# Low parts of weight tiles: an adding DMA in place of subtractions on VectorE and GpSimd

## The chip, the core and the metric

The kernel runs on one core of a Trainium2 chip. The metric is the device time of one execution, in microseconds (us). The profile names the engines: PE is TensorE (matrix products), with PEld for its weight loads; DVE is VectorE, ACT is ScalarE, POOL is GpSimd, and SP is the engine that issues the kernel's DMAs. Each engine works through its own queue in order.

## What is computed

One encoder block over 512 tokens and 16 meta tokens of width 1024, all in float32. Cut to what matters here:

```python
u = rms_norm(h, pre_mix_gain)
proj = u @ w_in                                # 1024 x 6656: qa, ka, va, qb, kb, vb, gates
o_swa  = windowed_gqa_sink_attention(rope(qa), rope(ka), va, sink)      # 16 query heads, 4 of K and V
o_diff = differential_attention(rope(qb), rope(kb), vb, lam)            # 8 heads, two softmaxes each
merged = sigmoid(g0) * (o_swa @ w_branch_swa) + sigmoid(g1) * (o_diff @ w_branch_diff)
h = h + rms_norm(merged @ w_out)
u = rms_norm(h, pre_ffn_gain)
f = (silu(u @ w_gate) * (u @ w_up)) @ w_ffn_out                         # hidden width 2816
out = h + rms_norm(f)
```

## The kernel before

**Two parts for each operand.** TensorE multiplies in a format with fewer mantissa bits (`float32r`). So every operand `x` of a large product is split into a high part, `hi = x` rounded to that format, and a low part, `lo = x - hi`. A product is `hi*hi + hi*lo + lo*hi`, three matmuls that accumulate in one bank (`mm3`, L139, its matmuls on L142, L143 and L144). The weight's low part is the stationary operand of L144.

**Weight tiles.** All weights pass through `load_w` (L124) in tiles of 128 x 1024, 512 KB each: 139 calls. SP issues a DMA from HBM into a raw tile `wr` (L126). ScalarE casts it into the high part `wh` (L130). The low part `wl` is `wr - wh` through `sub_hi` (L110, its instruction on L111). A counter `nw` numbers the calls. Calls 4 to 51 give three quarters of the columns (768) to GpSimd and one quarter (256) to VectorE; all others give all 1024 to VectorE. Raw tiles have `RB = 3` buffers, `wh` and `wl` three each (`wp`, L106). Some tiles have high and low parts of their own: the V tile of the windowed branch, `wV` (call 1), and the last two of each half of the FFN's second product (`xw`). Two tiles for the first K projection (`w_half`) and seven tiles of `w_out` are split by the helper `split` (L113) and not by `load_w`.

**Stages.** First x arrives slice by slice and is split, with the K and V projections of the windowed branch (`wV`, tile 1, then tile 2 for the second half of V). Then attention: streams for the windowed scores, their transposes and value products, the same for the differential branch, and a stream of fillers (projections for Q, K, V, gates, and `w_branch_swa`), which takes one weight tile after the other. `Order` (L35) lays down TensorE's order when the program is made, from fixed costs and delays (`LAT`); it does not depend on what the other engines do in the run. The other engines' orders come from the tile scheduler, except in the opening stage, where those of VectorE, ScalarE and SP follow the text. After attention come the product with `w_branch_diff` (8 tiles), `w_out` (8), the norm, and the FFN. Its first product (`ffn_in`) takes a gate tile and an up tile for each 128 hidden columns; the first three such pairs are run on each half of the tokens, 256 columns wide, while the norm of the other half is still under way (12 tiles), the other 19 pairs on all 512 (38 tiles). The second product takes 22 tiles.

**GpSimd's other work.** It adds the two halves of the rotary embedding (L327), scales the softmax rows (L476 and L636), makes the low part of squares in the differential norm (`split` with `eng=pool`), and does small steps of the norms (L164, L699 to L701). It issues no DMA. VectorE does the score reductions (L629 and L468), the combination of the two softmaxes (L635, L638), the rotary products (L325, L326) and most low parts of activations (L111, L119).

SP also issues the copies within the on-chip memory that regroup Q and K after the rotary embedding (tiles `Q`, `Qd`, `Kd`, `KK`, read from `hl`).

Of the kernel before, what the change touches and what calls it, by code (L numbers as in the profile page):

```python
"""Hybrid encoder block: windowed GQA with sink + differential attention, gated merge, SwiGLU FFN.

Every float32 operand of a large product is split exactly into two float32r parts (hi + lo);
a product is hi*hi + hi*lo + lo*hi accumulated in float32 in PSUM.
"""
# [29 lines left out]
class Order:  # L35
    """Order in which the tensor engine takes the work of several streams.

    A stream is a generator; it yields (cost, delay): the tensor time just traced and how long after
    it the stream's next piece has its operands, or a function that tells when (None: not yet) the
    next piece may follow. The first stream that is ready goes on."""  # L40

# [54 lines left out]
def encoder(ctx, tc, I, out, dbg=None):  # L96
# [11 lines left out]

# [1 line left out]
    def sub_hi(lo, src, hi, eng=None):  # L110
        (eng or dve).tensor_tensor(out=lo, in0=src, in1=hi.bitcast(F32), op=ALU.subtract)  # L111
# [12 lines left out]
    def load_w(src, k=KT, dst=None):  # L124
        raw = wp.tile([P, k, D // k], F32, tag="wr", name="wr", bufs=RB)
        sp.dma_start(out=raw, in_=src.rearrange("p (k c) -> p k c", k=k))  # L126
        if dst is None:
            dst = [wp.tile([P, k, D // k], F32R, tag=t, name=t) for t in ("wh", "wl")]
        wh, wl = dst
        act.copy(out=wh, in_=raw)  # L130
        # during attention the vector engine is the busiest: GpSimd takes three quarters of the low parts
        nw[0] += 1
        cut = 3 * k // 4 if 4 <= nw[0] < 52 else 0
        if cut:
            sub_hi(wl[:, 0:cut], raw[:, 0:cut], wh[:, 0:cut], pool)
        sub_hi(wl[:, cut:], raw[:, cut:], wh[:, cut:])
        return wh, wl
# [18 lines left out]
    def rsqrt_cols(pl, ss, n, scale, tag, extra=None, bufs=1):  # L156
        """(ss*scale + eps)^-0.5 on [n, m] columns, with one Newton step; extra replaces eps."""
        m = ss.shape[1]
        v, h, y, z = (pl.tile([P, m], F32, tag=tag + c, name=tag + c, bufs=bufs) for c in "vhyz")
        if extra is None:  # L160
            dve.tensor_scalar(out=v[:n], in0=ss, scalar1=scale, scalar2=EPS, op0=ALU.mult, op1=ALU.add)
        else:
            dve.scalar_tensor_tensor(out=v[:n], in0=ss, scalar=scale, in1=extra, op0=ALU.mult, op1=ALU.add)  # L163
        pool.tensor_tensor(out=y[:n], in0=v[:n], in1=mhalf[:n, 0:m], op=ALU.pow)  # L164
        dve.tensor_scalar(out=h[:n], in0=v[:n], scalar1=-0.5, scalar2=1.0, op0=ALU.mult, op1=ALU.mult)
        if m == 1:
            dve.scalar_tensor_tensor(out=z[:n], in0=y[:n], scalar=h[:n], in1=y[:n], op0=ALU.mult, op1=ALU.mult)
        else:
            dve.tensor_tensor(out=z[:n], in0=y[:n], in1=y[:n], op=ALU.mult)
            dve.tensor_tensor(out=z[:n], in0=z[:n], in1=h[:n], op=ALU.mult)  # L170
        dve.scalar_tensor_tensor(out=y[:n], in0=z[:n], scalar=1.5, in1=y[:n], op0=ALU.add, op1=ALU.mult)
        return y

# [1 line left out]
    ident = const.tile([P, P], F32, name="ident")  # L175
# [11 lines left out]
    mgain = vec[:, 0:8]  # L187
    zero = const.tile([P, 256], F32, name="zero")

    NB = 8  # L190
    LAT = dict(swa_q=13.52, swa_s=0.91, swa_p=3.9, tr=1.63, swa_o=1.66, v=1.7,
               diff_q=13.52, diff_s=2.1, norm=8.32, diff_p=4.2, rms=3.5, mp=0.75)
    RB = 3
    manual = tc.manual_schedule(engines={mybir.EngineType.PE})
# [16 lines left out]

    # the tensor engine's clock rises only under load
    warm = atp.tile([P, P], BF16, tag="rt", name="warm", bufs=4)
# [4 lines left out]

# [1 line left out]
    xh = big.tile([P, KT, EXT], F32R, tag="xh", name="xh")  # L220
# [50 lines left out]

    # K of the windowed branch, slice by slice as x arrives; then V
    Sw = ps.tile([P, 2, 512], F32, tag="S", name="Sw")
# [11 lines left out]

    # row statistics of x: 1/rms, broadcast to all partitions
    ss = const.tile([P, 5], F32, name="ss")
# [26 lines left out]

    # small vectors
    pool.tensor_scalar(out=hb, in0=vec[:, 8:24], scalar1=0.5, scalar2=1.0, op0=ALU.mult, op1=ALU.mult)
    pool.tensor_scalar(out=nsink, in0=vec[:, 24:40], scalar1=-1.0, scalar2=1.0, op0=ALU.mult, op1=ALU.mult)
    pool.tensor_scalar(out=g08, in0=vec[:, 40:41], scalar1=1.0 - LAMBDA_INIT, scalar2=1.0, op0=ALU.mult, op1=ALU.mult)

# [1 line left out]
    def rope(hl, psa, psb, c0, n, o0, scale=None):  # L321
        """psa, psb: [P, n] products of columns c0..c0+n; hl[:, part, hi/lo, o0..o0+n] gets the rotated split."""
        ta = atp.tile([P, 2, HALF], F32, tag="ta", name="ta", bufs=2)[:, :, 0:n]
        tb = atp.tile([P, 2, HALF], F32, tag="tb", name="tb")[:, :, 0:n]
        dve.tensor_tensor(out=ta, in0=psa.unsqueeze(1).broadcast_to([P, 2, n]), in1=rot[:, 1:3, c0:c0 + n], op=ALU.mult)  # L325
        dve.tensor_tensor(out=tb, in0=psb.unsqueeze(1).broadcast_to([P, 2, n]), in1=rot[:, 0:2, c0:c0 + n], op=ALU.mult)  # L326
        pool.tensor_tensor(out=ta, in0=ta, in1=tb, op=ALU.add)  # L327
        split(hl[:, :, 0, o0:o0 + n], hl[:, :, 1, o0:o0 + n], ta, scale=scale)
        return ta
# [29 lines left out]

# [1 line left out]
    def v_scale(VT, pv, h):  # L361
# [9 lines left out]

# [1 line left out]
    mk1 = atp.tile([P, 416], F32, tag="rt", name="mk1", bufs=4)  # L373
# [7 lines left out]
    def v_swa(VT):  # L381
# [5 lines left out]
        m = atp.tile([48, 2, 2, 64], F32R, tag="vm", name="Vm", bufs=2)  # L387
        act.copy(out=m, in_=zero[0:48, :].rearrange("p (a b c) -> p a b c", a=2, b=2))
        msrc = tm[0:NMETA, 0:P].rearrange("p (g e) -> p g e", g=2)
# [41 lines left out]

    # per query block: (key column range, mask, [(offset in range, key block or -1 for meta)])
    BLK = [
# [8 lines left out]

    # meta rows of the transposed probabilities; the gaps between the row groups stay zero
    aTm = atp.tile([80, 512], F32R, tag="am", name="aTm")
    for c in range(2):
        act.copy(out=aTm[:, c * 256:(c + 1) * 256], in_=zero[0:80, :])

# [35 lines left out]
    def pipe(n, tr_fn, av_fn, done_tr, free_at):  # L483
        """tr_fn(k), then av_fn(k, operand): two transposed banks ahead."""
        ready, ops = {}, {}
# [68 lines left out]

# [1 line left out]
    heads = {}  # L556
# [27 lines left out]
    def f_vd(h):  # L584
# [8 lines left out]
        def finish():  # L593
# [4 lines left out]
            m = atp.tile([80, P], F32R, tag="vm", name="Vdm", bufs=2)  # L598
            act.copy(out=m, in_=zero[0:80, 0:P])
            split(m[0:16], m[32:48], tm[0:NMETA, 0:P])  # L600
# [44 lines left out]
    def t_diff():  # L645
        free_at = 0.0
        for h in range(8):
# [27 lines left out]
            yield from pipe(5, tr_fn, av_fn, lambda: od.flag(("Ttd", h)), free_at)  # L675
            # per-head RMS norm over the 128 rows of O
            rt = lambda nm_, dt=F32: atp.tile([P, 512], dt, tag="rt", name=nm_, bufs=4)
# [28 lines left out]

# [1 line left out]
    t1 = big.tile([P, KT, NTOK], F32, tag="t1", name="t1")  # L708
# [8 lines left out]
    def f_tanh1():  # L717
        th = [act.activation(out=t1[:, j, :], in_=t1[:, j, :], func=AF.Tanh, scale=0.5, bias=hb[:, j:j + 1])
              for j in range(NB)]
        # one table set serves the Exp and the Ln of the differential branch  # L720
        behind(act.preload_act_table_set("natural_log_exp_and_others"), th)
        yield 0.0, 0.0
# [54 lines left out]

# [1 line left out]
    for j in range(KT):  # L779
# [13 lines left out]

    # the eight banks as two sets of four
    nb = {"acc": 0, "wk": 0}
# [13 lines left out]

# [1 line left out]
    gb01 = zp.tile([P, 2, D], F32, tag="kk", name="gb01", bufs=2)  # L811
# [7 lines left out]

    # all of w_out stays on chip, in the space of the hidden activations  # L820
    wo = [tl.tile([P, KT - 1, 2, 512], F32R, tag="hy%d" % c, name="wo") for c in range(2)]
# [81 lines left out]

# [1 line left out]
    hx = []  # L905
# [69 lines left out]

# [81 lines left out]
```

## Time and profile before

| what | value |
|---|---|
| time, median of 3 runs | 1016.11 us (1014.74 to 1017.35) |
| span of the profiled execution | 1015.2 us (first to last instruction; its own device time is not listed apart from the three runs) |
| instructions | 14301 |
| moved by DMA | 109.33 MB, 108 GB/s over the span |
| share of the 16 DMA engines' time, SP's queue | 35.3% |
| TensorE's granted clock, mean | 0.991 of full speed |

A profile is one execution. "Busy" is the time in which an engine had an instruction under way. The chain of waits is followed back from the last instruction, at each step to what released it. A group row gives an engine's instructions of one line and shape: busy time, mean duration in ns, and the idle time just ahead of them with what ended it. A row of a stage has the stretch, its length, busy time and count of PE, PEld, DVE, ACT and POOL in this order, then granted clock, share of the DMA engines, and GB/s.

### The profile page before, as it was taken

The page shows a single profiled execution, that of the slowest core. Times are in us where ns is not written, and L with a number is a line of the kernel's source. Part 1 is how long each engine was busy: PE and PEld are TensorE (multiplying, and loading weights), DVE is VectorE, ACT ScalarE, POOL GpSimd, SP SyncE. Part 2 cuts the span into 40 slices and gives each one's busy share as a digit, 9 for nine tenths or more (in the row PEclk, how much of TensorE's full clock was granted, in tenths as well). Part 3 has the DMA queues.
Part 4 walks back from the last instruction along what each step waited for, and adds up shares of the span by engine and source line. Part 5 has one row for each costly group of instructions (what it writes and reads, how often), then busy time and mean ns, then how long its engine had stood idle before and what let it go on. Part 6 is the DMA issues. An engine that isn't in the chain of part 4 may idle for free.

```text
span 1015.2 us, 14301 instructions
## 1 busy us (share of the span) xinstructions
PE 973.6 (96%) x5355; PEld 830.5 (82%) x5355; DVE 589.3 (58%) x979; ACT 446.8 (44%) x820; POOL 246.8 (24%) x294
## 2 busy tenths in 40 slices
PE   9989999989999997998999999999999999999997
PEld 9767777869888887988887888998888888888885
DVE  5856788766675868788874574863333333322224
ACT  6336677565443654654556352543233233222121
POOL 1443454534434554543421000100000000000000
PEclk9998999999999999998999999999999999999999
DMA  9572131341515144233512471353323323324122
GB/s 329 157 196 71 43 83 43 92 117 46 146 61 147 43 126 123 57 100 100 145 59 90 134 230 56 112 175 104 102 86 104 102 84 104 102 86 145 57 68 83
DMA packets 36597, 109.33 MB, mean 108 GB/s; under 512 B 5921, under 2 KB 6433, under 8 KB 35889
## 3 DMA queue, kind: packets, MB, share of 16 engines
q1 hardware_dynamic: 36528, 108.42, 35.3%
q8 instruction: 42, 0.69, 0.3%
q14 instruction: 27, 0.21, 0.1%
HBM read 87.04 MB, written 2.10 MB: 88 GB/s over the span
## 4 chain that ended last, share of the span: by engine, by line
PE 73%; DVE 12%; DMA 4%; issue 4%; ACT 4%; POOL 2%; SPq 1%; DVEq 0%; ACTq 0%; POOLq 0%
PE pr L142 15%; PE pr L143 15%; PE pr L144 15%; PE wk L142 2%; PE wk L143 2%; PE wk L144 2%; PE tr L516 2%; DMA wr<-in_w_in_dram 2%; PE Sd L626 2%; DVE wl L111 2%; PE Sw L465 2%; PE acc L143 1%; PE tr L143 1%; PE acc L142 1%; PE tr L142 1%
## 5 line engine op out<-in xcount | busy, mean ns | idle before, releaser
L130 ACT CAST wh<-wr 128x1024 fp32r<-128x1024 f32 x134 | 140.7, 1051 | 279.1 <-PE pr L143 122.2
L111 DVE TENSOR_TENSOR wl<-wr,wh 128x1024 fp32r<-128x1024 f32 (+2 forms) x138 | 153.1, 1110 | 138.3 <-ACT wh L130 130.5
L142 PE MATMUL pr<-xh,wh 128*128 128x264 f32 (+1 forms) x616 | 199.9, 325 | 0.0
L143 PE MATMUL pr<-xl,wh 128*128 128x264 f32 (+1 forms) x616 | 197.7, 321 | 0.7 <-DVE xl L234 0.7
L144 PE MATMUL pr<-xh,wl 128*128 128x264 f32 (+1 forms) x616 | 197.4, 320 | 0.7 <-DVE wl L111 0.7
L144 PEld LDWEIGHTS pr<-xh,wl 128*128 128x128 f32 x616 | 117.0, 190 | 9.3 <-DVE wl L111 0.9
L143 PEld LDWEIGHTS pr<-xl,wh 128*128 128x128 f32 x616 | 117.2, 190 | 7.1 <-DVE xl L234 1.2
L142 PEld LDWEIGHTS pr<-xh,wh 128*128 128x128 f32 x616 | 117.1, 190 | 6.9 <-issue 1.2
L111 POOL TENSOR_TENSOR wl<-wr,wh 128x768 fp32r<-128x768 f32 x48 | 95.6, 1992 | 86.9 <-ACT wh L130 85.0
L142 PE MATMUL pr<-uh,wh 128*128 128x512 f32 (+1 forms) x304 | 110.8, 364 | 0.0
L143 PE MATMUL pr<-ul,wh 128*128 128x512 f32 (+1 forms) x304 | 110.6, 364 | 0.0
L144 PE MATMUL pr<-uh,wl 128*128 128x512 f32 (+1 forms) x304 | 110.6, 364 | 0.0
L164 POOL TENSOR_TENSOR r3y<-r3v,mhalf 128x1 f32<-128x1 f32 x4 | 2.2, 552 | 352.7 <-DVE r3v L163 352.7
L142 PEld LDWEIGHTS pr<-uh,wh 128*128 128x128 f32 x304 | 57.3, 189 | 9.1
L144 PEld LDWEIGHTS pr<-uh,wl 128*128 128x128 f32 x304 | 57.4, 189 | 9.1
L143 PEld LDWEIGHTS pr<-ul,wh 128*128 128x128 f32 x304 | 57.4, 189 | 9.0
L629 DVE TENSOR_REDUCE dnm<-Sd 128x1 f32<-128x528 f32 x64 | 44.9, 702 | 22.8 <-PE Sd L626 22.5
L626 PE MATMUL Sd<-Kd,Qd 128*128 128x264 f32 x256 | 44.4, 295 | 9.6 <-ACT pp L630 8.0
L471 ACT ACTIVATE p<-p,nm 128x273 f32<-128x273 f32 (+1 forms) x64 | 36.9, 576 | 30.9 <-DVE nm L468 21.9
L468 DVE CUSTOM_DVE_ANT_0 p<-Sw,mk,nsink 128x272 f32<-128x272 f32 (+1 forms) x64 | 36.0, 563 | 24.3 <-PE Sw L465 22.9
L327 POOL TENSOR_TENSOR ta<-ta,tb 128x528 f32<-128x528 f32 (+1 forms) x26 | 35.7, 1372 | 55.0 <-DVE tb L326 46.4
L626 PEld LDWEIGHTS Sd<-Kd,Qd 128*128 128x128 f32 x256 | 36.7, 191 | 14.4 <-ACT pp L630 11.4
(370 smaller groups left out, 1979.3 us busy)
## 6 DMA issues: line engine op xcount, KB each, us to landing
wr<-in_w_in_dram SPq DMA_DIRECT2D x50, 512.0 KB, 3.8
wr<-in_w_fi_dram SPq DMA_DIRECT2D x50, 512.0 KB, 3.5
wr<-in_w_fo_dram SPq DMA_DIRECT2D x22, 512.0 KB, 3.5
Kd<-hl SPq DMA_DIRECT2D x32, 132.0 KB, 2.4
Kd<-Kd SPq DMA_DIRECT2D x8, 528.0 KB, 4.3
Q<-hl SPq DMA_DIRECT2D x64, 64.0 KB, 2.0
Qd<-hl SPq DMA_DIRECT2D x64, 64.0 KB, 2.1
wr<-in_w_bs_dram SPq DMA_DIRECT2D x8, 512.0 KB, 3.5
```

What stands on the lines that cost most here:

```text
L111: (eng or dve).tensor_tensor(out=lo, in0=src, in1=hi.bitcast(F32), op=ALU.subtract)
L130: act.copy(out=wh, in_=raw)
L142: pe.matmul(out=ps, lhsT=ah, rhs=bh, start=first, stop=False)
L143: pe.matmul(out=ps, lhsT=ah, rhs=bl, start=False, stop=False)
L144: pe.matmul(out=ps, lhsT=al, rhs=bh, start=False, stop=last)
L327: pool.tensor_tensor(out=ta, in0=ta, in1=tb, op=ALU.add)
L465: pe.matmul(out=S, lhsT=Qs[g][hh // 2][:, hh % 2, i * P:(i + 1) * P], rhs=KK[g // 2][:, c, g % 2, r0:r1], start=(c == 0), stop=(c == 1))
L468: dve.tensor_tensor_reduce(out=p[:, 0:nk], in0=S, in1=mask, scale=1.0, scalar=nsink[:, h:h + 1], op0=ALU.add, op1=ALU.min, accum_out=nm[:, ...
L471: act.activation(out=p, in_=p, func=AF.Exp, scale=-1.0, bias=nm[:, hh:hh + 1], accum_out=den[:, hh:hh + 1])
L516: pe.transpose(out=tr[0:kk, hh * P:(hh + 1) * P], in_=pt[:, hh, o:o + kk], identity=ident)
L626: pe.matmul(out=S[:, s, 0:HALF], lhsT=Q[:, c, i * P:(i + 1) * P], rhs=K[:, x, c, s * HALF:(s + 1) * HALF], start=(x == 0), stop=(x == 1))
L629: dve.tensor_reduce(out=nm[:, c:c + 1], in_=S[:, :, 0:HALF], axis=AX.XY, op=ALU.min)
```

## The change

`load_w` no longer subtracts. It writes the negated high part into `wl`, and then GpSimd issues a DMA that adds the raw tile to it in place: `wl = -wh + wr`. The negated high part comes from VectorE for calls 4 to 51 (a product of `wh` with -1), and from ScalarE for all others (a second pass over the raw tile with scale -1, rounded on output like the first). The DMA's destination is read as plain float32, so that nothing is rounded. It goes out on GpSimd's queue, waits there for the negated part, and TensorE's L144 matmuls wait for its landing. The raw tile is free for the next load when the addition has read it.

Two sizes change with it: `RB` goes from 3 to 4, and the tile of zeros goes from 256 columns to one, which its readers broadcast. Comments and docstrings were blanked without moving a line; behind `load_w`, which grew by one line, all line numbers are one higher.

```diff
@@ load_w
         act.copy(out=wh, in_=raw)
         nw[0] += 1
-        cut = 3 * k // 4 if 4 <= nw[0] < 52 else 0
-        if cut:
-            sub_hi(wl[:, 0:cut], raw[:, 0:cut], wh[:, 0:cut], pool)
-        sub_hi(wl[:, cut:], raw[:, cut:], wh[:, cut:])
+        if 4 <= nw[0] < 52:
+            dve.tensor_scalar(out=wl, in0=wh.bitcast(F32), scalar1=-1.0, scalar2=None, op0=ALU.mult)
+        else:
+            act.activation(out=wl, in_=raw, func=AF.Copy, scale=-1.0)
+        pool.dma_start(out=wl.bitcast(F32), in_=raw, accum_op=ALU.add)
         return wh, wl
@@ constants
-    zero = const.tile([P, 256], F32, name="zero")
+    zero = const.tile([P, 1], F32, name="zero")
...
-    RB = 3
+    RB = 4
@@ readers of zero (three places of this form)
-        act.copy(out=aTm[:, c * 256:(c + 1) * 256], in_=zero[0:80, :])
+        act.copy(out=aTm[:, c * 256:(c + 1) * 256], in_=zero[0:80].broadcast_to([80, 256]))
```

More of the change, by code (lines that the diff above doesn't have):

```diff
@@ L387, in v_swa @@
         m = atp.tile([48, 2, 2, 64], F32R, tag="vm", name="Vm", bufs=2)
-        act.copy(out=m, in_=zero[0:48, :].rearrange("p (a b c) -> p a b c", a=2, b=2))
+        act.copy(out=m, in_=zero[0:48].unsqueeze(2).unsqueeze(3).broadcast_to([48, 2, 2, 64]))
         msrc = tm[0:NMETA, 0:P].rearrange("p (g e) -> p g e", g=2)
@@ L598, in finish @@
             m = atp.tile([80, P], F32R, tag="vm", name="Vdm", bufs=2)
-            act.copy(out=m, in_=zero[0:80, 0:P])
+            act.copy(out=m, in_=zero[0:80].broadcast_to([80, P]))
             split(m[0:16], m[32:48], tm[0:NMETA, 0:P])
```

## The prediction

> **What bounds the kernel now.** I read the page's busy times and its chain first, then the busy times by stage, then what TensorE waited for in the attention stage, then the rows of the weight path, and last the timeline at the two places where weights follow each other fastest.
>
> ```profile
> span 1015.2 us, 14301 instructions
> PE 973.6 (96%) x5355; PEld 830.5 (82%) x5355; DVE 589.3 (58%) x979; ACT 446.8 (44%) x820; POOL 246.8 (24%) x294
> ...
> PE 73%; DVE 12%; DMA 4%; issue 4%; ACT 4%; POOL 2%; SPq 1%; DVEq 0%; ACTq 0%; POOLq 0%
> ```
>
> TensorE is busy for all but 41.6 us. The stages say where these are (columns: stretch, its length, the five engines' busy time, granted clock, DMA share, GB/s):
>
> ```profile
> 0.00:25.00 25.00, 23.18 (x204) 22.56 (x204) 13.20 (x25) 16.59 (x29) 3.92 (x24) 1.00 0.92 334
> 25.00:75.00 50.00, 44.69 (x221) 36.44 (x222) 36.02 (x64) 18.72 (x35) 23.27 (x17) 1.00 0.63 175
> 75.00:525.00 450.00, 422.43 (x2642) 366.15 (x2641) 334.88 (x608) 253.10 (x535) 205.88 (x235) 0.98 0.32 89
> 525.00:647.00 122.00, 121.83 (x560) 100.41 (x559) 71.47 (x116) 52.84 (x82) 10.41 (x12) 1.00 0.39 125
> 647.00:684.00 37.00, 37.00 (x304) 36.62 (x304) 25.78 (x39) 20.69 (x31) 1.10 (x2) 1.00 0.48 153
> 684.00:1000.00 316.00, 316.00 (x1396) 261.67 (x1395) 97.66 (x105) 82.06 (x103) 0.00 (x0) 1.00 0.29 92
> ```
>
> From 525 to 1000 us TensorE never stops: nothing that relieves another engine can gain there, and a new wait on weights costs its full length. The gain must come from the 450 us of attention, where 27.6 us are open. These are what TensorE waited for in that stretch (us in total, times, longest):
>
> ```profile
> PE Sd L626 <- ACT pp L630: 8.0, 7, 1.6
> PE O L534 <- DVE aTm L111: 4.5, 3, 2.1
> PE tr L658 <- DVE Vd L111: 3.5, 2, 2.0
> PE O L531 <- DVE al L111: 2.2, 4, 1.1
> PE Od L143 <- DVE dal L111: 2.0, 5, 0.8
> ```
>
> None of the five is a weight tile. They are results of VectorE (DVE), or of ScalarE (ACT) behind it: steps that came late because their engine's queue was long.
>
> **The change, part by part.** The low parts now cost this (busy us, mean ns of one, idle before):
>
> ```profile
> L130 ACT CAST wh<-wr 128x1024 fp32r<-128x1024 f32 x134 | 140.7, 1051 | 279.1 <-PE pr L143 122.2 <-issue 93.9 <-PE acc L144 28.5
> L111 DVE TENSOR_TENSOR wl<-wr,wh 128x1024 fp32r<-128x1024 f32 x86 | 107.2, 1246 | 127.3 <-ACT wh L130 124.2
> L111 DVE TENSOR_TENSOR wl<-wr,wh 128x256 fp32r<-128x256 f32 x48 | 43.3, 902 | 6.6 <-ACT wh L130 6.4 <-DMA Q<-hl 0.3
> L111 POOL TENSOR_TENSOR wl<-wr,wh 128x768 fp32r<-128x768 f32 x48 | 95.6, 1992 | 86.9 <-ACT wh L130 85.0
> ```
>
> *The negated copy.* For tiles 4 to 51 VectorE negates 1024 columns instead of subtracting 256; for the others ScalarE runs a second pass, which I price like its cast, 1.05 us. No row shows a 1024-column VectorE operation with one source. Short ones are in the trace beside a two-source one of their size, with the spread of those rows that meet GpSimd (POOL) traffic (ns, min/median/max):
>
> ```profile
> L601 DVE CAST Vdm<-Vdm x8: 218/219/420, 212.7 to 500.3; 16x128 fp32r<-16x128 f32 x8
> L111 DVE TENSOR_TENSOR Vdm<-tr,Vdm x8: 279/280/282, 212.5 to 500.0; 16x128 fp32r<-16x128 f32 x8
> L111 DVE TENSOR_TENSOR wl<-wr,wh x138: 408/1225/2514, 5.2 to 984.3; 128x1024 fp32r<-128x1024 f32 x86, 128x256 fp32r<-128x256 f32 x48, 128x512 fp32r<-128x512 f32 x4
> L635 DVE TENSOR_TENSOR drc<-drc,nlam x32: 147/160/1329, 263.4 to 530.6; 128x1 f32<-128x1 f32 x32
> L638 DVE SCALAR_TENSOR_TENSOR pa<-pp,drc,pa x24: 753/770/2352, 265.4 to 526.4; 128x528 f32<-128x528 f32 x24
> ...
> L638 DVE SCALAR_TENSOR_TENSOR pa<-pp,drc,pa 128x528 f32<-128x528 f32 x24 | 29.0, 1206 | 5.0 <-POOL pa L636 4.6
> L635 DVE TENSOR_TENSOR drc<-drc,nlam 128x1 f32<-128x1 f32 x32 | 17.1, 535 | 0.9
> ```
>
> Two sources cost (1225 - 408) / 768 = 1.06 ns a column and about 0.14 us besides; one source 219 ns for 128 columns, so near 0.6 ns a column. A negation of 1024 columns is then 0.14 + 0.6 = 0.75 us, between 0.7 and 1.23 (the full two-source row). I take 0.75, because the cast has the same types and one source.
>
> *What the port waits give back.* The 256-column piece takes 0.41 us at best and 0.90 on average: half of it waits for GpSimd. The same shows in the one-column product (0.54 on average against 0.16) and in the combination of the two softmaxes (1.21 against 0.77). These two groups lose 32 x 0.375 + 24 x 0.436 = 22.5 us. GpSimd's subtractions are 95.6 of its 205.9 us in this stage; if the waits fall in that proportion, the two groups lose 10 us less, and the 0.49 us wait of the piece becomes 0.26. The negations then cost 48 x 1.01 = 48.5 us where the pieces cost 43.3, so VectorE ends about 5 us lighter of 335. GpSimd drops 95.6 us and takes 48 issues.
>
> *The issue on GpSimd.* No DMA is issued from there in this trace. SP's issues take 0.33 us (row below); above stands the 1.99 us that the issue replaces. I take the middle, 1.2 us: 48 x 1.2 = 58 us, so GpSimd is 38 us lighter, a fifth of its stage. [...]
>
> *The new wait.* The issue stands in GpSimd's in-order queue until the negation is done. Behind it stand the rotary additions (L327, ScalarE's scaling waits for them) and the softmax scalings (L476, L636, VectorE waits for the second). Until now GpSimd waited there for the cast alone; it now waits 0.75 us more and is done 0.8 us sooner, which I put at nothing. If VectorE's queue holds the negation back by its own length, it is 0.75 us for each of 48.
>
> *Worth in attention.* No row says how much of the 27.6 us follows the two queues; the ends are 0 and 27.6. GpSimd is a fifth lighter and VectorE barely, so I take a fifth, -6 us.
>
> *The adding transfer.* It is the part that the trace shows least:
>
> ```profile
> wr<-in_w_fi_dram SPq DMA_DIRECT2D x50, 512.0 KB, 3.5
> Kd<-Kd SPq DMA_DIRECT2D x8, 528.0 KB, 4.3
> L126 SPq DMA_DIRECT2D wr<-in_w_fi_dram x50: 327/328/328, 600.2 to 858.4; - x50
> ```
>
> A load of 512 KB lands 3.5 us after issue. At the 334 GB/s of the first 25 us its bytes take 1.6 us, so 1.9 us are fixed. The addition has two tiles to read, 3.1 us, so 5.1 us; with 1.2 for the issue in place of 0.33 it lands 5.9 us after GpSimd begins. The lower end is a plain load, 4.4 by the same exchange; the upper end two whole copies within SBUF and the longest issue, 2 x 4.3 + 2.0 = 10.6. I take 5.9, since the load is the transfer with the same 128 rows.
>
> *First tiles, +6.* The tile of the first V projection is number 1, without cover (start, length, what ran; brackets: idle before it and what ended it):
>
> ```profile
> 15.57 1.05 ACT L130 CAST wV<-wr 128x1024 fp32r<-128x1024 f32 x1 [2.05 <-DMA wr<-in_w_in_dram]
> 19.04 0.19 PEld L144 LDWEIGHTS tr<-xh,wV 128*128 128x128 f32 x1
> 24.65 1.05 ACT L130 CAST wh<-wr 128x1024 fp32r<-128x1024 f32 x1 [0.93 <-DMA wr<-in_w_in_dram]
> 27.00 0.19 PEld L144 LDWEIGHTS pr<-xh,wl 128*128 128x128 f32 x1 [0.88 <-DVE wl L111]
> ```
>
> Cast and second pass end at 17.7, the addition lands at 23.6, and TensorE wants the low part at 19.04: 4.5 us. Tile 2 lands at 24.65, is ready at 24.65 + 2.1 + 5.9 = 32.7, and is wanted at 26.1 + 4.5: 2.0 us where 0.88 stand now. That makes 5.6, and 6 with a DMA share of 0.92 in the way. Ends: 4 and 12.
>
> *The narrow FFN tiles, +7.* Between 647 and 684 us twelve tiles meet 256 columns each, and ScalarE's casts show their pace:
>
> ```profile
> 658.12 1.05 ACT L130 CAST wh<-wr 128x1024 fp32r<-128x1024 f32 x1 [1.59 <-issue]
> 659.08 0.40 ACT L115 CAST hx<-sg 128x256 fp32r<-128x256 f32 x1
> 661.00 1.05 ACT L130 CAST wh<-wr 128x1024 fp32r<-128x1024 f32 x1 [1.52 <-issue]
> ```
>
> A tile lasts 2.88 us. With three buffers of the parts, a buffer that falls free is wanted again two tiles later, in 5.76 us. Now it takes 1.05 + 1.25; then it takes 2.1 + 5.9 = 8.0, so it comes 2.24 us late every third tile, 0.75 us a tile. Three of the twelve are ready beforehand: 9 x 0.75 = 7. Ends: 9 x 0.25 = 2 and 9 x 2.3 = 21. The four raw buffers last 11.5 us, just what load, passes and addition need. ScalarE rises from 20.7 to 33.3 of 37 us; that cover is thin.
>
> *The wide tiles, 0.* From 684 to 1000 us a tile lasts 316 / (1396 / 24) = 5.43 us, so 10.9 us are there for 8.0. The transfers hide with 2.9 us to spare, and the DMA share goes from 0.29 to about 0.87, if an addition counts twice. Should the cover be gone, each of some 56 tiles (those outside the narrow stage, without the last four, which have buffers of their own) pays a third of what is over. Between 525 and 647 us the same spacing holds, and ScalarE has 69 us free for 16 more passes. The fourth raw buffer and the smaller zero tile cost nothing by themselves.
>
> Sum: +6 - 6 + 7 = +7 us, 1022 on the span of 1015.2 and **1023 us** on the median of 1016.11; the span lies 0.9 us under that median, and I add the same to both.
>
> **The rivals.**
>
> *Not slower: the queues were the stalls (31%).* If the port waits of VectorE, 46 us over the groups above (23.5 in the pieces, 22.5 in the two others), sit right ahead of the late results, taking GpSimd's subtractions away removes most of the open time in attention. The maxima speak for it: a 0.16 us product that took 1.33 is a queue held up in the middle of a softmax. Against it: the pieces give way to negations which meet the remaining 110 us of GpSimd work. From 16 us of the 27.6 on it outweighs the other terms by 3 us; with 20 of them the time is 1016 + 6 - 20 + 7 = 1009.
>
> *Level: the addition is as quick as a load (20%).* With 4.4 us from the start of the issue, the first tiles cost 3.0 + 1.1 and the narrow ones 9 x 0.25 = 2, against -6: 1016. For it: a copy within SBUF, whose bytes are the same in number, is only 0.8 us above a load. [...]
>
> *Much slower: the addition outlasts its cover (17%).* Above 10.9 - 2.1 = 8.8 us from issue to landing, the wide tiles stall. At 9.5 us they lose 56 x 0.23 = 13 us, the narrow ones 9 x 1.95 = 17, the first 9 + 1: 1016 + 13 + 17 + 10 - 6 = 1050. For it: two whole copies within SBUF would take 8.6 us with no issue counted, and the DMA share comes near 1; against it: the loads leave 71% of the engines' time free.
>
> **How the numbers follow.** The forecast has 32%, the rivals 31, 20 and 17. About 0.3%, 3 us, is what a measurement of this kernel tells from no change. Faster 0.31, same 0.20, slower 0.32 + 0.17 = 0.49. The forecast's own range runs from 1019 to 1040 (first tiles +12, narrow +15, attention -3). The range over all cases ends at 1002, where all 27.6 us are gone beside the forecast's other terms (1016 + 13 - 27.6), and at 1057, the third rival with a landing at 9.8 us (wide tiles 56 x 0.33 = 19, narrow 9 x 2.05 = 18, first 10, attention -6); I leave a tenth to either side.
>
> **What would show it.** In the profile after: the negation near 0.75 us (1.23 would put VectorE 23 us higher); the issue on GpSimd near 1.2; the landing near 5 to 6. TensorE should wait for a low part at 19 us for about 4.5, and in the narrow stage for 2 us every third tile. Its stretch from 684 to 1000 should stay full, and its open time in attention fall from 27.6 to about 22. The forecast is wrong if the landing is under 4.5 us, or if the open time falls under 12, or if the wide tiles wait.

## The result and the profile after

The changed kernel takes 1099.1 us (median of four runs, 1098.12 to 1101.51) where the kernel before takes 1016.65 (four runs, 1014.74 to 1017.35) beside it: a ratio of 1.0814, 95% interval 1.0792 to 1.0836. The forecast was 1023 us with a range up to 1057. The direction was right, the size was not.

The page of the changed kernel, first its busy times, then its two DMA queues (packets, MB, share of the 16 engines' time), then the chain of waits:

```profile
span 1099.7 us, 14560 instructions
PE 999.9 (91%) x5355; PEld 847.2 (77%) x5355; DVE 458.5 (42%) x888; ACT 530.9 (48%) x911; POOL 271.2 (25%) x385
...
q0 software_dynamic: 20016, 72.88, 36.4%
q1 hardware_dynamic: 36528, 108.42, 32.2%
...
PE 35%; DMA 15%; issue 9%; DVE 4%; SPq 3%; ACT 3%; POOL 2%; DVEq 0%; POOLq 0%; ACTq 0%
```

Three readings. VectorE lost 131 us of work, as meant. TensorE does the same 5355 products in the same order, and yet it is both open for longer (99.8 us, before 41.6) and busy for longer (999.9, before 973.6): of the 84.5 us, 58 are waiting and 26 are products that ran slower. And the additions, 139 tiles, took 36.4% of 16 engines: 0.364 x 1099.7 / 139 = 2.9 us of all engines for each 512 KB, while the 108.42 MB of everything else took 354 us, 1.7 us for 512 KB. The transfers went from 4% of the chain to 15%.

What TensorE waited for, over the whole run (us in total, times, longest):

```profile
PE Sd L627 <- DMA Qd<-hl: 21.4, 6, 6.6
PE pr L145 <- DMA wl<-wr: 13.5, 10, 2.8
PE Sw L466 <- DMA Q<-hl: 8.1, 2, 7.9
...
PE tr L145 <- DMA wV<-wr: 7.3, 1, 7.3
...
PE acc L144 <- DMA wl<-wr: 4.5, 2, 3.5
PE tr L144 <- DMA wl<-wr: 3.4, 1, 3.4
```

The four rows of low parts are new, 28.7 us together (two smaller ones, left out, add 4.5). But the largest is no weight tile: it is `Qd`, the copies that regroup Q for a head of the differential branch, for which TensorE waited 0.3 us in the whole run of before; `Q`, the same for the windowed branch, went from 2.7 to 8.1. The change does not touch them. The DMA issues show what became of them (KB each, median us from issue to landing), before and after:

```profile
Kd<-hl SPq DMA_DIRECT2D x32, 132.0 KB, 2.4
Qd<-hl SPq DMA_DIRECT2D x64, 64.0 KB, 2.1
```

```profile
wl<-wr POOLq DMA_DIRECT2D x134, 512.0 KB, 5.9
wr<-in_w_fi_dram SPq DMA_DIRECT2D x50, 512.0 KB, 5.0
Kd<-hl SPq DMA_DIRECT2D x32, 132.0 KB, 5.5
Qd<-hl SPq DMA_DIRECT2D x64, 64.0 KB, 4.7
wV<-wr POOLq DMA_DIRECT2D x1, 512.0 KB, 8.8
```

The addition lands in 5.9 us, as forecast. But a 132 KB copy beside it takes 5.5 us instead of 2.4, and a load of the FFN's weights 5.0 instead of 3.5. One head shows what that does. These are the rows of SP's queue for head 4, before and after (start, length, what was issued), and the additions of that time on GpSimd:

```profile
393.69 2.56 SPq L572 DMA_DIRECT2D Kd<-hl  x4
...
398.08 0.50 SPq L574 DMA_DIRECT2D Kd<-Kd  x1
398.62 3.25 SPq L579 DMA_DIRECT2D Qd<-hl  x3
```

```profile
417.55 3.77 SPq L573 DMA_DIRECT2D Kd<-hl  x4
...
424.28 0.50 SPq L575 DMA_DIRECT2D Kd<-Kd  x1
424.82 4.00 SPq L580 DMA_DIRECT2D Qd<-hl  x3
```

```profile
416.47 0.89 POOL L137 DMA_DIRECT2D wl<-wr  x1 [1.20 <-PE Sd L627]
...
421.82 0.88 POOL L137 DMA_DIRECT2D wl<-wr  x1 [1.80 <-issue]
```

After the rotary step come four copies into `Kd`, a copy of `Kd` onto its other half, the last three copies into `Qd`, then the head's first score product: before, 9.0 us from the first `Kd` issue to that product (393.7 to 402.7). After, 12.6 (417.5 to 430.1). Both additions shown start while this head's copies are under way. In the trace of before none of the 32 `Kd<-hl` copies had a load under way beside it; after, all 32 had an addition beside them, and 17 a load as well.

### The profile page after: what moved, and what is told of

It is laid out like the page before. It is cut to its first block, busy times and chain, and to the rows that moved or that the text cites. A ratio compares the mean times of both kernels' runs of the same rounds, so it can differ in the third digit from the quotient of the medians.

```text
span 1099.7 us, 14560 instructions
## 1 busy us (share of the span) xinstructions
PE 999.9 (91%) x5355; PEld 847.2 (77%) x5355; DVE 458.5 (42%) x888; ACT 530.9 (48%) x911; POOL 271.2 (25%) x385
## 3 DMA queue, kind: packets, MB, share of 16 engines
q0 software_dynamic: 20016, 72.88, 36.4%
q1 hardware_dynamic: 36528, 108.42, 32.2%
## 4 chain that ended last, share of the span: by engine, by line
PE 35%; DMA 15%; issue 9%; DVE 4%; SPq 3%; ACT 3%; POOL 2%; DVEq 0%; POOLq 0%; ACTq 0%
PE pr L145 8%; PE pr L144 8%; PE pr L143 8%; DMA wl<-wr 6%; DMA Kd<-hl 3%; DMA Qd<-hl 2%; DMA wr<-in_w_fo_dram 2%; PE wk L144 2%; PE wk L143 2%; PE wk L145 2%; PE Sd L627 2%; SPq L573 1%; SPq L580 1%; DMA wr<-in_w_out_dram 1%; POOL wl L137 1%
## 5 line engine op out<-in xcount | busy, mean ns | idle before, releaser
L137 POOL DMA_DIRECT2D wl<-wr x134 | 117.7, 879 | 522.0 <-ACT wl L136 341.1
L144 PE MATMUL pr<-xl,wh 128*128 128x264 f32 (+1 forms) x616 | 199.2, 323 | 0.1
L144 PEld LDWEIGHTS pr<-xl,wh 128*128 128x128 f32 x616 | 118.6, 193 | 6.5 <-DVE xl L235 0.5
L136 ACT ACTIVATE wl<-wr 128x1024 fp32r<-128x1024 f32 x86 | 90.5, 1052 | 43.6 <-PE acc L144 19.1
L144 PE MATMUL pr<-ul,wh 128*128 128x512 f32 (+1 forms) x304 | 110.9, 365 | 0.0
L627 PE MATMUL Sd<-Kd,Qd 128*128 128x264 f32 x256 | 47.2, 309 | 31.1 <-DMA Qd<-hl 21.4
L145 PEld LDWEIGHTS pr<-uh,wl 128*128 128x128 f32 x304 | 57.6, 189 | 18.4 <-DMA wl<-wr 9.5
L144 PEld LDWEIGHTS pr<-ul,wh 128*128 128x128 f32 x304 | 57.7, 190 | 9.1
L134 DVE TENSOR_SCALAR wl<-wh 128x1024 fp32r<-128x1024 f32 x48 | 42.3, 880 | 14.0 <-ACT wh L130 13.9
```

The costliest lines, as they stand in the source:

```text
L134: dve.tensor_scalar(out=wl, in0=wh.bitcast(F32), scalar1=-1.0, scalar2=None, op0=ALU.mult)
L136: act.activation(out=wl, in_=raw, func=AF.Copy, scale=-1.0)
L137: pool.dma_start(out=wl.bitcast(F32), in_=raw, accum_op=ALU.add)
L144: pe.matmul(out=ps, lhsT=ah, rhs=bl, start=False, stop=False)
L145: pe.matmul(out=ps, lhsT=al, rhs=bh, start=False, stop=last)
L627: pe.matmul(out=S[:, s, 0:HALF], lhsT=Q[:, c, i * P:(i + 1) * P], rhs=K[:, x, c, s * HALF:(s + 1) * HALF], start=(x == 0), stop=(x == 1))
```

## The experiments

Each run was timed beside the kernel before on its own chip; that kernel's medians there were 1016.2 to 1016.6 us, close enough to compare the runs with each other too. Line numbers of these kernels are up to six higher than the changed kernel's; the tiles' names tell the rows apart.

**1. A plain copy in place of the addition.** The low part is then the raw tile: the addition is left out, every issue, wait and pass stays.

```diff
-        pool.dma_start(out=wl.bitcast(F32), in_=raw, accum_op=ALU.add)
+        pool.dma_start(out=wl.bitcast(F32), in_=raw)
```

> Leaves out the addition: GpSimd's DMA overwrites the negated high part with the raw tile, so the low part is wrong and the bytes read fall by half. Theory A (the second read keeps the DMA engines busy, and loads and regroup copies queue behind it): the landing falls from 5.9 to about 4.4 us, the Kd copies from 5.5 to about 3.5, the software queue's share from 36% to about 20%, and the time goes halfway back, to 1055 to 1065. Rival B (the hop through another queue is what costs, whatever it reads): landing and copies fall by less than 0.5 us and the time stays within 10 of 1099.

1037.3 us (ratio 1.0202, 1.0171 to 1.0233). Its DMA page:

```profile
q0 software_dynamic: 20016, 72.88, 18.1%
wl<-wr POOLq DMA_DIRECT2D x134, 512.0 KB, 3.4
Kd<-hl SPq DMA_DIRECT2D x32, 132.0 KB, 4.7
```

With as many bytes to write, the copies take half the engine time (18.1% of 1036 us, 1.35 us a tile), land in 3.4 us instead of 5.9, and cost 21 us instead of 82. So 62 of the 82 us belong to the adding form: its doubled engine time, its later landing, its longer issue (0.88 us against 0.55). They do not belong to a second DMA per tile as such or to its place in the queues. More came back than expected (1055 to 1065 us), although the `Kd` copies stayed slow, 4.7 us where about 3.5 were expected.

TensorE takes the same products in the same order in all these kernels, so their starts can be compared one by one. In this run it is 6.9 us behind the kernel before at that kernel's 106th us, 6.4 at its 525th, 8.0 at its 647th, and 20.6 from its 684th on. The plain copy thus costs time in the opening and with the narrow tiles, and none in attention or in the second FFN product.

**2 to 4. The change by stages.** Additions in tiles 4 to 51 alone; from 52 on alone; none at all with the two sizes of the change (`RB = 4` and the zero tile of one column).

```diff
 # 2: low parts of tiles 1-3 and 52-139
+            sub_hi(wl, raw, wh)
 # 3: low parts of tiles 1-51 as in the kernel before
 # 4: all low parts as in the kernel before
+        cut = 3 * k // 4 if 4 <= nw[0] < 52 else 0
+        if cut:
+            sub_hi(wl[:, 0:cut], raw[:, 0:cut], wh[:, 0:cut], pool)
+        sub_hi(wl[:, cut:], raw[:, cut:], wh[:, cut:])
```

> Tiles 4 to 51 as after, all others subtracted on VectorE. If the loss adds up by stages (the lag of TensorE's order behind the kernel before: 24 us by the first scores, 8 back in the windowed part, 28 in the differential part, 38 behind attention), the time is 1016 + 24 - 8 + 28, less some 14 of the opening's 24 that tiles 1 to 3 caused: 1045 to 1060. If the stages trade (time lost in one is given back in the next), it lies outside, under 1040 or over 1070.

> Tiles 1 to 51 subtracted as before, tile 52 on as after. By the stages' sum 1016 + 38 = 1054 (13 around w_branch_diff and w_out, 11 in the narrow tiles, 14 at the two ends of the FFN's second product), 1045 to 1060. If the fourth raw buffer alone helps or hurts, it shifts by what the fourth run of this set shows. The forecast's chain (7 for the narrow tiles and nothing else) would give 1023.

> All subtractions as before, with four raw buffers and the one-column zero tile. If the windowed part's 8 us come from the fourth raw buffer, the time is 1008 to 1012; if they come from lighter VectorE and GpSimd, it is 1016 within 3. If the order of SP's queue that the fourth buffer brings costs the opening stage its 24 us, it is over 1025.

They took 1039.2 us (1.0247, 1.0209 to 1.0286), 1053.6 (1.0373, 1.0338 to 1.0408) and 1013.6 (0.9976, 0.9962 to 0.999). The sizes alone gain 2.6 us, and this fourth kernel is the fastest of all that ran, ahead of both. Run 3 came out as expected. Run 2 lies below its range of 1045 to 1060 us, on the side where time lost in one stage is partly given back in another. Run 4 was to tell why TensorE catches up some 8 us in the windowed half of the changed kernel: 1008 to 1012 us would have spoken for the fourth buffer, 1013 to 1019 for the lighter engines; it lies at the edge of the second. Against it the additions of attention cost 25.5 us, those from tile 52 on 40.0, and 20 are left for tiles 1 to 3.

**5. Tiles 1 to 3 subtracted.**

```diff
+        if nw[0] < 4:
+            sub_hi(wl, raw, wh)
+            return wh, wl
```

> The changed kernel, but tiles 1 to 3 have their low parts subtracted on VectorE. Against the kernel with subtractions and four raw buffers (1013.6 us), additions in tiles 4 to 51 alone cost 25.5 us and additions from tile 52 on 40.0 us, which leaves 20 of the 85.5 us for tiles 1 to 3. Theory: that is the opening, where TensorE waits 7 us for the low part of the first V tile and SP's in-order queue holds the small loads behind raw tiles that only a landed addition releases. Expected 1076 to 1083 us, with TensorE less than 8 us behind the kernel before at its 100th us. Rival: the stages are not additive (a late start is absorbed in attention, where the steps wait for other engines anyway). Then 1090 us or more.

1084.3 us (1.0662, 1.0624 to 1.07): 14.8 us less than the changed kernel, a little short of the expectation. At the kernel before's 100th us TensorE is 2.7 us behind it, where the changed kernel is 18.4 behind.

**6. Only the windowed half of attention, tiles 4 to 19.**

> Additions in tiles 4 to 19 alone (the windowed half of attention), all others subtracted as before, four raw buffers. Theory: in attention the additions cost time only where the regroup copies of a differential head stand between its projection and its first score product; the windowed half has slack for its own copies. Expected 1013 to 1018 us, beside 1013.6 without additions. Rival: each addition of the attention stage costs about the same (25.5 us over 48 tiles), so 16 tiles cost 8.5 us: 1022 us. A third way: the relief of GpSimd and VectorE shows once nothing opposes it, and the time falls to 1010 or less.

1018.5 us (1.0011, 0.9998 to 1.0025), just above the expectation, and 4.9 above the kernel without additions; the 32 of the differential half cost the other 20.7. The 4.9 us are not spread over the 16 tiles. They lie before the 100th us, at the copies that regroup Q and K for the first windowed heads, which the theory took to have slack:

```profile
PE Sw L472 <- DMA Q<-hl: 8.9, 3, 7.2
```

Run 4 has 3.5 us there, 2.9 at the longest, and its 136 KB copies into `KK` land in 2.8 us, here in 6.2. The relief of the engines did not show as a gain in the total.

**7. Only the wide tiles, 80 to 117.**

> Additions in tiles 80 to 117 alone (the 38 wide tiles of the FFN's first product), all others subtracted as before, four raw buffers. Theory, and a step of the prediction: these transfers hide, since a tile lasts 5.43 us and load, passes and addition are done in time. Expected 1013 to 1016 us, beside 1013.6 without additions. Rival: the 86 additions from tile 52 on cost evenly (40 us), so 38 of them cost 18 us: 1031 us.

1014.5 us (0.9987, 0.9973 to 1.0): 0.9 us for 38 additions. They hide.

**8. A shorter chain of copies.** On top of run 2, the lower half of `Kd` is copied from `hl` by ScalarE's queue, and the copy of the finished half goes.

```diff
+                act.dma_start(out=K[64 + 32 * i:96 + 32 * i, :, c, :].bitcast(F32),
+                              in_=hl[64 + 32 * c:96 + 32 * c, i, :, 0:EXT].bitcast(F32))
...
-        sp.dma_start(out=K[64:128].bitcast(F32), in_=K[0:64].bitcast(F32))
```

> Additions in tiles 4 to 51 alone, as in the run that took 1039.2 us, but the lower half of each head's K tile is filled by four copies from the rotated tile, issued from ScalarE's queue beside SP's, and no longer by one copy of the finished upper half. Theory: in the differential half the time is lost in the chain of copies from the last rotary step to a head's first score product, which the additions stretch from 9 to 12 us to 12 to 17 us; a chain without its second link is some 4 us shorter per head, so most of the 18 us that TensorE waited for the query copies goes: expected 1022 to 1031 us. Rival: the loss is in the DMA engines' total load or in ScalarE's and VectorE's queues; then taking a link out changes nothing, or the 32 issues on ScalarE cost something: 1036 to 1045 us.

1046.5 us (1.0298, 1.0266 to 1.0329): a miss, 7 us slower than run 2. What TensorE waited for, and the new copies (KB, landing):

```profile
PE Sd L628 <- ACT pp L632: 14.2, 5, 5.7
...
PE Sd L628 <- DMA Qd<-hl: 2.3, 1, 2.3
```

```profile
Kd<-hl ACTq DMA_DIRECT2D x32, 132.0 KB, 6.0
Kd<-hl SPq DMA_DIRECT2D x32, 132.0 KB, 5.4
```

The wait for `Qd` did go, from 18.0 us in run 2 to 2.3. But the issues hold ScalarE's queue 1.23 us each at the median, and the exponentials behind them (`pp`) come late instead: 14.2 us where run 2 had 6.1. The copies on a second queue land as slowly as those on SP's, so standing in SP's queue alone does not explain their pace; but there are twice as many 132 KB copies now. This run does not tell how much a shorter chain is worth.

**9 and 10. The additions that meet the copies, and the others.** In run 2, 19 of the 32 tiles of the differential half had their addition under way during a head's copies. One kernel adds these alone, the other the remaining 13.

```diff
+        if nw[0] not in (21, 22, 26, 27, 28, 29, 34, 35, 36, 39, 40, 41, 42, 43, 44, 46, 47, 49, 50):
 # 10: (20, 23, 24, 25, 30, 31, 32, 33, 37, 38, 45, 48, 51)
```

> In the run with additions in tiles 4 to 51, 19 tiles of the differential half (21, 22, 26 to 29, 34 to 36, 39 to 44, 46, 47, 49, 50) had an addition under way while a head's regroup copies were. Here these 19 are added and all other tiles subtracted as before, four raw buffers. Theory: the loss of that half (some 20 us) comes from those meetings, so it is nearly all here: expected 1029 to 1036 us beside 1013.6 without additions, with copies of Kd landing near 5 us after issue. Rival: each addition of that half costs the same, 20 us over 32, and 19 cost 12 us: 1023 to 1027 us.

> The other 13 tiles of the differential half (20, 23 to 25, 30 to 33, 37, 38, 45, 48, 51), whose additions met no regroup copies, are added and all other tiles subtracted as before, four raw buffers. Theory of the meetings: no loss, 1011 to 1017 us, with copies of Kd landing near 2.4 us. Rival of an even cost: 8 us, so 1020 to 1024 us.

1028.1 us (1.0116, 1.0089 to 1.0143) and 1017.7 (1.001, 0.9996 to 1.0025). Both lie between the two theories' numbers, on the side of the meetings for run 9: 14.5 us for 19 additions (0.76 each) against 4.1 for 13 (0.32 each). Their landings, first run 9, then run 10:

```profile
wl<-wr POOLq DMA_DIRECT2D x19, 512.0 KB, 5.4
Kd<-hl SPq DMA_DIRECT2D x32, 132.0 KB, 4.6
```

```profile
wl<-wr POOLq DMA_DIRECT2D x13, 512.0 KB, 4.6
Kd<-hl SPq DMA_DIRECT2D x32, 132.0 KB, 3.6
```

In run 9 TensorE waited 13.9 us for `Qd`, in run 10 never, and 2.8 us for `Kd`. The heads' chains tell it directly. From the first `Kd` issue to the head's first score product, the last six heads took 66.4 us together in run 4, 66.9 in run 10, 79.6 in run 9, 83.7 in the changed kernel, and 70.0 with the plain copies of run 1. So run 9's loss is nearly all in the heads whose copies met additions.

That run 10 still loses 4 us has a hint in its second row: no addition met a `Kd` copy, but a load did in 23 of 32 cases (none without additions), since the next load into a raw tile waits for its addition to land and moves with it (in the changed kernel SP waited 665.2 us for such landings, 102 times). TensorE's wait for `Kd` is 1.8 us longer than in run 4; where the rest of the 4 us lies is not shown.

**11. The opening's queue.** One load, the lambda vectors, moved ahead of the tiles that wait.

```diff
     sp.dma_start(out=rot, in_=I["rot"])
+    lt = atp.tile([P, 4, 64], F32, tag="rt", name="lt", bufs=4)
+    sp.dma_start(out=lt, in_=I["lam"])
```

> The changed kernel with one load moved: the four lambda vectors are loaded ahead of the tiles that wait for a landed addition, right behind the rotary table, so that VectorE's lambda products and the rotary step of K behind them do not stand behind SP's queue. Theory: of the 15 us that the additions of tiles 1 to 3 cost, some 8 belong to the low part of the first V tile and the rest to this queue: expected 1089 to 1094 us beside 1099.1. Rival: the opening waits for the copies of K and for the additions themselves, whose pace the load does not change: 1096 to 1101 us.

1088.4 us (1.0712, 1.0684 to 1.074): 10.7 us gained by moving 128 KB, slightly more than expected. SP's queue shows why, in the kernel before and in the changed one:

```profile
15.63 2.86 SPq L126 DMA_DIRECT2D wr<-in_w_in_dram  x3
25.57 0.33 SPq L350 DMA_DIRECT2D lt<-in_lam_dram  x1
```

```profile
15.97 27.45 SPq L126 DMA_DIRECT2D wr<-in_w_in_dram  x7
43.53 0.36 SPq L351 DMA_DIRECT2D lt<-in_lam_dram  x1
```

Seven weight loads stand ahead of `lt` in the changed kernel, the later ones waiting for a raw tile that only a landed addition sets free (not, as the section on the change has it, one that has read the tile): between 14 and 45 us SP waited 8.3 us for the landing in `wV` and 14.6 us for three in `wl`. In run 4, with the same four buffers, four loads stood ahead and `lt` went out at 25.6 us. VectorE takes its work in order and waits 8.3 us for `lt`:

```profile
47.16 0.23 DVE L355 CUSTOM_DVE_ANT_0 lj<-lt 128x64 f32<-128x64 f32 x1 [8.29 <-DMA lt<-in_lam_dram]
```

Behind it stands the rotary step of K, whose addition on GpSimd starts at 48.9 us instead of 33.7, and the scaling of V, for which TensorE waited 7.3 us in the opening of the changed kernel and 0.9 in run 11.

**12. Negation on VectorE from tile 52 on**, on top of run 3:

```diff
-            act.activation(out=wl, in_=raw, func=AF.Copy, scale=-1.0)
+            dve.tensor_scalar(out=wl, in0=wh.bitcast(F32), scalar1=-1.0, scalar2=None, op0=ALU.mult)
```

> Additions from tile 52 on, as in the run that took 1053.6 us, but VectorE writes the negated part (0.7 us, one pass over the high part) in place of ScalarE (1.05 us). Theory, the prediction's step for the narrow tiles: a buffer's round of passes and landing outlasts the two tiles that cover it; the round is only 0.35 us shorter, so little changes: 1048 to 1054 us, and TensorE still waits 10 us or more for low parts in the narrow stage. Rival: ScalarE was the limit there (33 of 37 us if nothing waited), and taking 12.6 us of passes away frees the stage: 1036 to 1044 us.

1049.9 us (1.0334, 1.0308 to 1.0361), as the theory said, though TensorE waited only 8.7 us for low parts in the narrow stage, not 10 or more. ScalarE was not the limit of the narrow stage.

**13 to 15. The 40 us from tile 52 on.** Narrow tiles alone (68 to 79); tiles 80 to 139; the same without the four tiles that have buffers of their own.

```diff
 # 13: added only if 68 <= nw[0] < 80    14: only if nw[0] >= 80
 # 15: as 14, but not 127, 128, 138, 139
```

> Additions in tiles 68 to 79 alone (the twelve narrow tiles of the FFN's first product), all others subtracted as before, four raw buffers. Theory: the narrow stage by itself loses what TensorE fell behind there in the run with additions from tile 52 on, 13 to 15 us, so 1025 to 1030 us beside 1013.6 without additions. Rival: there the stage was reached with buffers already late, after the product with the output weights; from a clean start it loses what the prediction said, 7 us: 1018 to 1023 us.

> Additions from tile 80 on (wide tiles of the first product and all of the second), all others subtracted as before, four raw buffers. Theory: the two ends of the second product lose what TensorE fell behind there in the run with additions from tile 52 on, 10 to 12 us: 1024 to 1027 us, beside 1014.5 with the wide tiles alone. Rival: the lag at the ends was carried over from earlier stages: 1014 to 1018 us.

> The same without the four tiles that have buffers of their own (the last two of each half of the second product, 127, 128, 138, 139), which VectorE subtracts. Theory: at each end four additions are issued within 5 us, two of these tiles' and two ordinary ones, and the DMA engines serve all of them late; with two of the four left the wait goes: 1014 to 1018 us. Rival: a tile of the second product has no spare time, whoever adds beside it: 1021 to 1026 us, nearly as with all of them.

1027.2 us (1.0113, 1.0084 to 1.0141), 1024.3 (1.0075, 1.0047 to 1.0102) and 1019.4 (1.003, 1.0012 to 1.0049). The narrow stage costs 13.6 us by itself. The second product costs 9.8 beyond the wide tiles, and half of it goes with the four tiles of the burst: run 15 (ten runs from 1015.0 to 1023.3) lies between its two theories. TensorE's waits in run 14 from 900 us on:

```profile
PE acc L150 <- DMA wl<-wr: 4.5, 2, 3.3
PE pr L150 <- DMA wl<-wr: 2.4, 1, 2.4
```

Without the four tiles the first row is gone and the second stays.

The shares add up like this:

| part of the change | us | from |
|---|---|---|
| the two sizes | -2.6 | run 4 |
| tiles 1 to 3 (opening) | 14.8 | changed kernel less run 5 |
| tiles 4 to 51 (attention) | 25.5 | run 2 less run 4 |
| tiles 52 to 67 (the last seven of `w_in`, `w_branch_diff`, one of `w_out`) | 15.7 | run 3 less runs 13 and 14 |
| tiles 68 to 79 (narrow) | 13.6 | run 13 less run 4 |
| tiles 80 to 117 (wide) | 0.9 | run 7 less run 4 |
| tiles 118 to 139 (second FFN product) | 9.8 | run 14 less run 7 |

The parts sum to 77.7 us of 82.5; the rest is in what one stage does to the next, and in the medians. The 15.7 us are a remainder: no run had these tiles alone.

## Why the prediction was wrong, step by step

**The operations were priced nearly rightly, one of them by luck.** Their rows after (busy us, mean ns, idle before):

```profile
L137 POOL DMA_DIRECT2D wl<-wr x134 | 117.7, 879 | 522.0 <-ACT wl L136 341.1 <-issue 27.5 <-PE Sw L466 24.2
L136 ACT ACTIVATE wl<-wr 128x1024 fp32r<-128x1024 f32 x86 | 90.5, 1052 | 43.6 <-PE acc L144 19.1 <-PE pr L144 14.8 <-DMA wr<-in_w_fo_dram 9.6
L134 DVE TENSOR_SCALAR wl<-wh 128x1024 fp32r<-128x1024 f32 x48 | 42.3, 880 | 14.0 <-ACT wh L130 13.9
L639 DVE SCALAR_TENSOR_TENSOR pa<-pp,drc,pa 128x528 f32<-128x528 f32 x24 | 24.4, 1015 | 6.0 <-POOL pa L637 5.9
L636 DVE TENSOR_TENSOR drc<-drc,nlam 128x1 f32<-128x1 f32 x32 | 9.3, 290 | 1.0
```

Negation 0.88 us (1.01 predicted), ScalarE's pass 1.05 (1.05), issue 0.88 (1.2), landing 5.9 (5.9). The landing is right by luck: the prediction built 5.9 us for an addition by itself, and that takes 4.5 (the least of the 134); among the kernel's other transfers the median is 5.9. What the prediction calls port waits is shown as a longer VectorE operation beside a GpSimd one: in the trace of before, the 43 pieces of 256 columns with GpSimd at work beside them took 0.96 us on the mean, the five without 0.41. No run shows what holds it. The last two groups gave back 24 x 0.19 + 32 x 0.245 = 12.4 us of it where 10 were forecast.

**The wide tiles, 0: right.** Two stretches of the changed kernel, the narrow tiles and the wide ones (columns as in the prediction's stages):

```profile
700.00:757.00 57.00, 46.88 (x339) 43.83 (x338) 15.83 (x37) 34.99 (x51) 11.50 (x15) 0.97 0.85 203
757.00:975.00 218.00, 218.00 (x963) 180.52 (x962) 26.36 (x39) 99.13 (x118) 35.43 (x41) 1.00 0.87 196
```

The second row has TensorE full and the DMA share at 0.87, the very number of the prediction.

**Worth in attention, -6: the step that failed by kind.** It took over the relief of VectorE and GpSimd and charged the additions nothing beyond their own landing. Measured: +25.5, of which 4.9 in the windowed half. No run's total showed the relief: with additions in one half alone, or only where they met no copies (runs 6 and 10), the time was 4 to 5 us above the kernel without them. Within a trace there is some: in run 9 TensorE is 3.3 us ahead of run 4 from the 220th to the 320th us of the kernel before, ahead of the first loss. The prediction counted every step that waits for an addition and none that shares the DMA engines with one. The regroup copies were the place: a chain of small transfers that TensorE waits for, with nothing to spare (before, it waited 1.4 us for those of the differential branch in all). In run 8 the copies landed late on SP's queue (5.4 us) and on ScalarE's (6.0) alike; no run shows how the DMA engines divide their time between queues.

**First tiles, +6: measured 14.8.** TensorE's wait for `wV` came out at 7.3 (4.5 predicted), because this addition landed in 8.8 us amid the loads of x and of the next weights (DMA share 0.93 up to 25 us). The larger part, 10.7 us by run 11, was a transfer that nobody had priced: a small load behind seven weight loads in SP's in-order queue. The two overlap, since together they come to more than 14.8.

**Narrow tiles, +7: measured 13.6, inside its ends of 2 to 21.** The mechanism held, two sizes did not. TensorE's waits in the stage, run 13:

```profile
PE pr L151 <- DMA wl<-wr: 7.4, 4, 4.2
PE wk L151 <- DMA wl<-wr: 3.1, 2, 1.8
```

These are 10.5 us. The round of a buffer, from the start of the cast to the landing, took 9.1 us on the mean of the last nine tiles, not 8.0; by the prediction's own form, (9.1 - 5.76) / 3 = 1.1 us, over its nine tiles, 10 us. The rest of the loss is products that ran slower, a term the prediction did not have: the granted clock was 0.93 from 647 to 697 us, where it was 1.00 before. Why the round is longer is argued, not shown: a load and an addition take 1.7 + 2.9 = 4.6 us of all 16 engines, and a narrow tile lasts 2.88, so they cannot keep up. In run 1, with 1.7 + 1.35 = 3.05 us of engine time a tile and a round of 7.2, TensorE still fell 12.6 us further behind there. So which of the two limits binds, the serial round or the engines' rate, stays open. For a wide tile, 4.6 of 5.43 us is 0.85, which fits that stage holding.

**"Between 525 and 647 us the same spacing holds": wrong, up to 15.7 us.** Seven of the 16 tiles that the prediction put there belong to the end of attention. In run 3's trace TensorE falls 7 us behind run 4 by the 530th us, where the first of these additions meet the last head's copies, and 9 us more by the 647th. The additions of that stretch meet the gain vectors' and `w_out`'s loads: in the changed kernel two of those beside them, at 581 and 627 us, landed in 9.1 and 10.8 us, and TensorE waited for low parts of the products with `w_branch_diff` and `w_out`, 3.4 us at the longest. **The second product was never a step: 9.8 us.** At the end of each half four additions and their loads come together; between 1000 and 1012 us the engines had no time left (the view's share is 1.04) and TensorE lost 3.5 of the 12 us:

```profile
1000.00:1012.00 12.00, 8.46 (x30) 6.58 (x31) 0.00 (x0) 3.98 (x4) 1.72 (x2) 0.86 1.04 269
```

**The clock was no step either.** Each stall was priced at its length. This is TensorE in the narrow stage after a 2.63 us wait, from the timeline (start, length; rows left out):

```profile
724.07 0.39 PE L145 MATMUL pr<-uh,wl 128*128 128x256 f32 x1 [2.63 <-DMA wl<-wr]
724.29 0.28 PE L143 MATMUL pr<-uh,wh 128*128 128x256 f32 x1
724.41 0.28 PE L144 MATMUL pr<-ul,wh 128*128 128x256 f32 x1
...
727.60 0.41 PE L145 MATMUL pr<-uh,wl 128*128 128x256 f32 x1
727.82 0.41 PE L143 MATMUL pr<-uh,wh 128*128 128x256 f32 x1
```

The starts follow each other by 0.12 us right after the wait, by 0.215 from about 725.1 to 728.7, and by 0.12 again: some 3.5 us at 0.56 of the speed, 1.5 us lost on top of 2.6. The granted clock from 725.3 to 728.6 us was 0.50; it was 0.50 from 646.8 to 650.1 us as well, after a wait of 2.1 us. Not every wait was followed by this: one of 2.8 us lies between 742 and 748 us, and the clock was 1.00 from 742 to 754. No run shows what lowers it. Over the run the granted clock fell from 0.991 to 0.963, and the busy time rose by the 26 us seen above: 0.45 us more for each us of added waiting.

**The rivals.** "Level: as quick as a load" had nearly the right price, 4.4 us, for an addition that meets little: 4.6 us in run 10. It is the crowd that makes it 5.9: in run 9, whose additions met the copies, it was 5.4. "Much slower" named the wide tiles as the place, which were the one place that held (its first tiles, 9 + 1, come to 8 + 1 by the prediction's own form). "Not slower" counted on port waits, which did fall (by the 12.4 us above), and no run's total shows a gain from it.

## What to carry to other kernels

Here a transfer's price was its own landing, 5.9 us, and also what it did to the others in flight: the `Kd` copies went from 2.4 to 5.5 us, the loads of the FFN's first product from 3.5 to 5.0. Before moving work onto the DMA engines, list the small transfers that the critical engine waits for, and see which of them the new ones will meet. Compare the engines' time per tile (here 4.6 us) with the time that a tile lasts, stage by stage: a mean share of 0.35 said nothing of the stages with 2.88 us tiles and of the bursts at the seams. Where a buffer's release moves onto a transfer, look at what stands behind its next filling in an in-order queue: here `lt` was issued at 43.5 us in place of 25.6. In this kernel each us of added waiting of TensorE came with another 0.45 us of slower products.

## What was not expected of the hardware

- An adding DMA within the on-chip memory takes 2.9 us of the 16 engines for 512 KB, a plain copy of the same tile 1.35: more than double.
- The adding form also holds GpSimd longer for its issue: 0.88 us against 0.55 for the plain copy.
- The issue of a 132 KB copy of 32 partitions on SP went from 0.60 us to 1.07 at the median in the changed kernel (0.64 in run 2, with the additions of attention alone), and on ScalarE, in run 8, such an issue took 1.23 us. No run shows what holds it.
